# The last SwiGLU on the undivided residual with a turned result, and pools padded to multiples of 1 KB

## The chip, the cores and the metric

The kernel runs on one core of a Trainium2 chip. The metric is the device time of one execution in microseconds (us). Everything is computed in float32: the large products take their operands in a rounded form of it (fp32r below), split into a high and a low part.

## The reference

A backbone of two layers over 256 latent and 256 context tokens of 1,024 channels. Each layer is a half SwiGLU, a mixer and a second half SwiGLU. What matters here is the second SwiGLU of the last layer, for latent tokens alone, and the norm behind it:

```python
def rmsnorm(x, g):
    y = x * rsqrt(mean(x * x, axis=-1) + NORM_EPS)
    return y * g
def modulate(h, shift, scale):
    return h * (1 + scale) + shift
def swiglu(h, w_gate, w_up, w_down):
    return (silu(h @ w_gate) * (h @ w_up)) @ w_down
...
        lat = lat + m_lat[:, :, 5] * y_lat                     # y_lat: the odd mixer's out projection
        lat = lat + 0.5 * gate * swiglu(modulate(rmsnorm(lat, g), shift, scale), *ffn2)
    return rmsnorm(lat, final_norm)                            # (1, 256, 1024)
```

The inner size of a SwiGLU is 2,816, that is 22 tiles of 128.

## The kernel before, in words

Channels lie on the 128 partitions and tokens along the free dimension. The residual `res` has eight channel tiles of 512 columns: 256 context tokens (CTX), then 256 latent ones (LAT). Every product with weights goes through `mm3` (L152 to 161): for each tile of 128 input channels three matmuls, high weight by high x (L158), high weight by low x (L159), low weight by high x (L160). A column block of weights is loaded by SP into a `raw` tile, cast on ScalarE (L148) and its remainder taken on VectorE (L149). Four raw and four weight tiles rotate. The first three SwiGLU passes, the input projections and most of the rest run over 512 columns, the last SwiGLU over 256.

A SwiGLU (`ffn`, L437) first norms its input: the sum of squares over channels is kept in `acc` by `stat` (ScalarE squares, VectorE adds, L291 and L292). `rstd_stats` sums it over the partitions by a matmul with a column (L253), VectorE takes the inverse root in nine small steps (L260 to L269), and `rstd_rows` turns the two columns into a row on all partitions (matmul with the identity, L278). Then `norm_tile` makes each of the eight x tiles (L309, L314, L316), and the gate and up products follow. Inner tiles come in groups of 6, 8 and 8; behind each group `down` multiplies them by the down weights, eight blocks of output channels, and `residual` (L429) adds each block to `res`. Accumulators rotate through six banks of PSUM (`pm`), two more (`ps`) serve the norms.

`final` takes the norm's row again, multiplies each of the eight tiles by gain and row on VectorE (L1266), and sends it out on SP's queue (L1269). The result leaves with channels on partitions, (8, 128, 256), and is turned on the host.

Each engine works through its own queue in order. The order is set by a scheduler while the kernel is built, from the code's order, priorities (`high_priority`) and its own estimates. Tiles live in pools; a pool's slots lie side by side, and those of a stage (`phase`) start behind the constants, the weight tiles and the small tiles (`cst`, `rawp`, `wp`, `sm`).

Of the kernel before, what the change touches and what calls it, by code (L numbers as in the profile page):

```python
# [9 lines left out]
F32 = mybir.dt.float32  # L10
F32R = mybir.dt.float32r
I32 = mybir.dt.int32
AF = mybir.ActivationFunctionType
ALU = mybir.AluOpType
# [4 lines left out]
P = 128  # L19
D = 1024  # L20
KT = D // P
NTOK = 256
T2 = 2 * NTOK
F = 2816
NF = F // P
CHUNKS = ((0, 6), (6, 14), (14, 22))
# [7 lines left out]
SOON = 100  # L34
# [13 lines left out]
CTX, LAT = (0, NTOK), (NTOK, T2)  # L48
# [17 lines left out]
class Builder:  # L66
    def __init__(self, tc, ctx, t, out):
        self.tc, self.nc, self.t, self.out = tc, tc.nc, t, out
        pool = lambda name, bufs, **kw: ctx.enter_context(tc.tile_pool(name=name, bufs=bufs, **kw))
        self.cst = pool("cst", 1)  # L70
        self.rawp = pool("rawp", 4)
        self.wp = pool("wp", 4)
        self.sm = pool("sm", 4)
        self.pmm = pool("pmm", 6, space=PSUM)
        self.psm = pool("psm", 2, space=PSUM)
        self.dram = pool("dram", 1, space=DRAM)
        self.n = 0
        self.bg = []
        self.stage = None
        self.last_act = None  # L80
        self.keep = tc.keep_in_program_order

    def uid(self, s):
# [342 lines left out]
    def residual(self, i, ps, gate, h, last):  # L426
        c0, c1 = h
        r = self.res[:, i, c0:c1]
        self.nc.vector.scalar_tensor_tensor(  # L429
            r, ps[:, c0:c1], gate[:, i, VEC[h] : VEC[h] + 1], r, op0=ALU.mult, op1=ALU.add  # L430
        )
        if last:
            self.stat(i, h)


    def blocks(self, idx, n=3):
# [2 lines left out]
    def ffn(self, l, k, halves, after=None, spare=None, lead=None):  # L439
        nc, t = self.nc, self.t  # L440
        idx = 2 * l + k // 2
        lo, hi = halves[0][0], halves[-1][1]
        wgu = t["wgu"][idx]
        xs, pss = self.norm_proj(l, k, halves, self.blocks(idx, 4 if lead else 3), lead, spare if len(halves) > 1 else None)
        if lead is not None:
            self.mod_setup()
            self.start(self.mod_job((0, m) for m in (2, 3, 4, 5, 6, 7)), 1.6)
        for f0, f1 in CHUNKS:
            hid = []
            for f in range(f0, f1):  # L450
                for g in range(2):
                    if 2 * f + g == len(pss):
                        pss.append(self.pm())
                        w = self.wload(wgu[f, g], D)
                        self.mm3(pss[-1][:, lo:hi], self.wparts(w, KT), self.parts(xs, lo, hi))
                pg, pu = pss[2 * f : 2 * f + 2]
                s = self.slot("h", [P, 2, T2])
                nc.scalar.activation(s[:, 0, lo:hi], pg[:, lo:hi], AF.Silu)  # L458
                nc.vector.tensor_mul(s[:, 1, lo:hi], s[:, 0, lo:hi], pu[:, lo:hi])  # L459
                hd = self.slot("h", [P, 2, T2], F32R)  # L460
                self.split(hd[:, 0, lo:hi], hd[:, 1, lo:hi], s[:, 1, lo:hi])
                hid.append(hd)
                self.tick(2)
            gate = self.need(l, 3 * k + 2)
            self.down(lambda i: t["wd"][idx, i][:, f0 * P : f1 * P], hid, gate, halves, f1 == NF, f1 - f0, after)

    def proj(self, name, blk, xs, c0, c1):
        w = self.wload(self.t[name][blk], D)
        ps = self.pm()
        self.mm3(ps[:, c0:c1], self.wparts(w, KT), self.parts(xs, c0, c1))  # L470
        return ps
# [630 lines left out]
    def odd_mixer(self):  # L1102
        nc, t = self.nc, self.t
# [4 lines left out]
        xs, pss = self.norm_proj(1, 1, both, [t["od_in"][i] for i in ODD], spare="g")  # L1108
# [8 lines left out]
        for i in range(4):  # L1117
            ps = pss[i]
# [17 lines left out]
        for i in range(4):  # L1136
            ps = self.proj("od_in", 16 + i, xs, *LAT)
            nc.scalar.activation(lg[:, i], ps[:, N:T2], AF.Gelu_apprx_tanh)
        gates = {}
        for i in range(4):  # L1140
# [3 lines left out]
            for d in range(2):  # L1144
                ra = gates[i, d] = self.slot("g", [P, 2, T2])
                for g in range(2):
                    ps = self.pm()
# [100 lines left out]
        for i in range(4):  # L1248
            ps = self.pm()
            for f in range(4):  # L1250
                src = (yr if f < 2 else yi)[:, f % 2, i * P : (i + 1) * P]
                nc.tensor.matmul(ps[:, :N], lhsT=src, rhs=idft[:, f, :], start=f == 0, stop=f == 3)
            z = self.slot("hy", [P, N])
            v.scalar_tensor_tensor(z, uu[:, i], hb[:, i : i + 1], ps[:, :N], op0=ALU.mult, op1=ALU.add)
            v.tensor_mul(z, z, x0[:, i])
            o = self.slot("x", [P, 2, T2], F32R)
            self.split(o[:, 0, N:T2], o[:, 1, N:T2], z)
            os.append(o)
        self.out_proj("od_out", 1, os, [LAT])

    def final(self):
        nc = self.nc
        self.rb[LAT] = self.rstd([self.acc[LAT]], self.inv_d)
        for i in range(KT):
            y = self.slot("h", [P, NTOK])
            nc.vector.scalar_tensor_tensor(  # L1266
                y, self.res[:, i, NTOK:T2], self.gain[:, 6, i : i + 1], self.rb[LAT], op0=ALU.mult, op1=ALU.mult
            )
            nc.sync.dma_start(self.out[i], y)  # L1269

    def build(self):
        nc, t = self.nc, self.t
# [1 line left out]
        self.acc, self.rb, self.mod = {}, {}, {}  # L1274
        self.res = self.const([P, KT, T2], "res")
        s5p = dict.fromkeys(("sb0", "sb1", "pa", "pb", "bank", "tm", "mb", "mbt", "vt", "et"), 1)
        self.phase(x=8, **s5p, gs=2, sc=1, junk=1, m=2, ct=1, h=10)
        self.ct = self.slot("ct", [P, KT, 32])
        for i in range(0, KT, 2):
            nc.sync.dma_start(self.res[:, i : i + 2, :], t["xt"][:, i : i + 2, :])  # L1280
# [16 lines left out]
        for i in range(KT):  # L1297
            if i == 6:
                w = self.slot("sc", [P, 2, 4, 2 * P])
# [27 lines left out]
        self.drain()  # L1327
        self.phase(x=8, g=8, lx=2, hy=13)
        self.odd_mixer()
        self.phase(x=8, h=10)  # L1330
        self.ffn(1, 2, [LAT])
        self.final()
        self.stage.close()

# [158 lines left out]
```

## Time and profile before

| | |
|---|---|
| median of 3 runs | 1797.6 us (1797.04 to 1797.97) |
| the profiled execution | 1795.22 us, of which 1793.4 span |
| mean granted TensorE clock | 0.986 |
| TensorE busy | 1727.7 us, 96% of the span |
| VectorE busy | 1252.9 us, 70% |
| ScalarE busy | 684.1 us, 38% |
| last layer's second SwiGLU | about 1584 to 1781 us |

The span runs from the first to the last instruction; the execution's own time is 1.8 us longer. Matmuls are pipelined: one that takes 282 ns in the profile starts 119 ns after the one ahead of it, so the distance of the starts is the cost, and a busy TensorE isn't one at its peak. A line such as "PE mm L158" is the matmul of line 158 that writes a tile named mm.

### The profile page before, as it was taken

Reading aid. Unit: us, or ns where it says so; the run is one execution under the profiler, and the core shown is the slowest. Engines: PE = TensorE matmul, PEld = TensorE weight load, DVE = VectorE, ACT = ScalarE, POOL = GpSimd, SP = SyncE. Lnnn points to the kernel's source line nnn. Section 1 sums busy time; section 2 is a strip of 40 time slices with the busy share of each in tenths; the row PEclk is TensorE's granted clock in tenths of the full one; section 3 lists DMA queues with packets and bytes.
Section 4 is the critical chain, followed back from the end, with each engine's and each line's share of the span. In section 5 each row is a group of like instructions: output and inputs, shape, how many; then the busy total and the mean of one; then the engine's idle time right before and its main releaser. Section 6 shows DMA issues by size and latency. Waiting matters only on the chain.

```text
span 1793.4 us, 24725 instructions
## 1 busy us (share of the span) xinstructions
PE 1727.7 (96%) x9364; PEld 1444.7 (81%) x9364; DVE 1252.9 (70%) x2464; ACT 684.1 (38%) x1082; POOL 13.2 (1%) x47
## 2 busy tenths in 40 slices
PE   5999999999989999999999999999999999789997
PEld 3778777779868788778888888888888888589997
DVE  7999999987488668776666686544543576875555
ACT  4433333343445653222222233222122357554442
POOL 0000000000000000000000000000000000000000
PEclk9999999999998999999999999999999999799999
DMA  9566666652465453464454544555433225146552
GB/s 324 173 216 211 223 214 216 210 189 90 125 185 172 120 189 115 154 223 152 147 183 153 164 130 130 179 173 163 156 117 95 94 94 201 49 150 191 183 185 92
DMA packets 108055, 292.63 MB, mean 163 GB/s; under 512 B 21216, under 2 KB 36448, under 8 KB 107680
## 3 DMA queue, kind: packets, MB, share of 16 engines
q1 hardware_dynamic: 102368, 287.39, 49.8%
q10 hardware_dynamic: 4928, 2.10, 0.7%
q8 instruction: 73, 1.20, 0.3%
q0 software_dynamic: 640, 1.57, 0.3%
q14 instruction: 46, 0.38, 0.1%
HBM read 272.20 MB, written 18.28 MB: 162 GB/s over the span
## 4 chain that ended last, share of the span: by engine, by line
PE 87%; DVE 7%; DMA 2%; ACT 1%; issue 1%; SPq 1%; DVEq 0%; ACTq 0%
PE mm L158 25%; PE mm L160 25%; PE mm L159 25%; PE mm L155 6%; DVE w L149 1%; DMA h<-in_modw_dram 1%; PE mm L1148 1%; SPq L981 1%; DVE nt L309 1%; DMA x<-d_g 1%; DVE x L316 1%; DMA x<-d_v 0%; PE ps L278 0%; PE ps L631 0%; PE ps L1059 0%
## 5 line engine op out<-in xcount | busy, mean ns | idle before, releaser
L159 PE MATMUL mm<-x,w 128*128 128x512 f32 (+1 forms) x1600 | 575.1, 360 | 0.0
L160 PE MATMUL mm<-x,w 128*128 128x512 f32 (+1 forms) x1600 | 574.5, 360 | 0.0
L158 PE MATMUL mm<-x,w 128*128 128x512 f32 (+1 forms) x1600 | 569.4, 361 | 4.5 <-ACT x L314 3.3
L148 ACT CAST w<-raw 128x1024 fp32r<-128x1024 f32 (+2 forms) x324 | 328.5, 1018 | 527.7 <-issue 254.1
L149 DVE TENSOR_TENSOR w<-raw,w 128x1024 fp32r<-128x1024 f32 (+2 forms) x324 | 384.0, 1187 | 191.7 <-ACT w L148 190.8
L158 PEld LDWEIGHTS mm<-x,w 128*128 128x128 f32 x1600 | 300.9, 189 | 55.9 <-ACT x L314 3.9
L159 PEld LDWEIGHTS mm<-x,w 128*128 128x128 f32 x1600 | 301.8, 189 | 48.9 <-issue 2.0
L160 PEld LDWEIGHTS mm<-x,w 128*128 128x128 f32 x1600 | 301.8, 189 | 48.7 <-issue 1.2
L225 DVE CUSTOM_DVE_ANT_0 junk<-m,sc 128x1024 f32<-128x1024 f32 x224 | 273.3, 1220 | 1.8 <-DMA m<-in_modw_dram 0.2
L158 PE MATMUL mm<-h,w 128*128 128x512 f32 (+1 forms) x632 | 229.2, 367 | 0.0
L160 PE MATMUL mm<-h,w 128*128 128x512 f32 (+1 forms) x632 | 228.4, 364 | 0.0
L159 PE MATMUL mm<-h,w 128*128 128x512 f32 (+1 forms) x632 | 228.3, 363 | 0.0
L429 DVE SCALAR_TENSOR_TENSOR res<-mm,mraw,res 128x256 f32<-128x256 f32 x192 | 86.1, 480 | 103.7 <-PE mm L160 92.8
L459 DVE TENSOR_TENSOR h<-h,mm 128x512 f32<-128x512 f32 (+1 forms) x88 | 54.6, 621 | 128.5 <-PE mm L160 111.0
L458 ACT ACTIVATE h<-mm 128x512 f32<-128x512 f32 (+1 forms) x88 | 48.0, 545 | 234.5 <-PE mm L160 223.7
L159 PEld LDWEIGHTS mm<-h,w 128*128 128x128 f32 x632 | 119.1, 188 | 20.6 <-issue 1.0
L158 PEld LDWEIGHTS mm<-h,w 128*128 128x128 f32 x632 | 118.6, 188 | 21.0 <-issue 1.1
L160 PEld LDWEIGHTS mm<-h,w 128*128 128x128 f32 x632 | 118.9, 188 | 20.5 <-issue 0.6
L155 PE MATMUL mm<-x,w 128*128 128x256 f32 x384 | 66.1, 289 | 6.7 <-DVE x L316 6.2
L314 ACT ACTIVATE x<-nt,mraw 128x256 fp32r<-128x256 f32 x88 | 42.9, 506 | 54.5 <-DVE nt L309 54.5
L155 PEld LDWEIGHTS mm<-x,w 128*128 128x128 f32 x384 | 53.9, 188 | 11.6 <-DVE x L316 9.2
L165 DVE TENSOR_TENSOR h<-h,h 128x512 fp32r<-128x512 f32 (+1 forms) x88 | 54.5, 619 | 0.0
(345 smaller groups left out, 1604.5 us busy)
## 6 DMA issues: line engine op xcount, KB each, us to landing
raw<-in_wgu_dram SPq DMA_DIRECT2D x176, 512.0 KB, 3.8
m<-in_modw_dram SPq DMA_DIRECT2D x130, 512.0 KB, 4.3
raw<-in_wd_dram SPq DMA_DIRECT2D x64, 512.0 KB, 3.6
raw<-in_wd_dram SPq DMA_DIRECT2D x32, 384.0 KB, 3.3
raw<-in_od_in_dram SPq DMA_DIRECT2D x20, 512.0 KB, 3.5
h<-in_modw_dram SPq DMA_DIRECT2D x12, 512.0 KB, 9.9
raw<-in_ev_in_dram SPq DMA_DIRECT2D x10, 512.0 KB, 3.5
d_mb<-mbt SPq DMA_DIRECT2D x16, 256.0 KB, 2.9
```

The costliest lines, as they stand in the source:

```text
L148: nc.scalar.copy(hi[:, :n], raw[:, :n])
L149: nc.vector.tensor_sub(lo[:, :n], raw[:, :n], hi[:, :n])
L155: mm = lambda *a, **k: self.keep(self.nc.tensor.matmul(*a, **k))
L158: mm(ps, lhsT=wh, rhs=xh, start=first and i == 0, stop=False)
L159: mm(ps, lhsT=wh, rhs=xl, start=False, stop=False)
L160: r = mm(ps, lhsT=wl, rhs=xh, start=False, stop=last and i == n - 1)
L165: self.nc.vector.tensor_sub(lo, src, hi)
L225: nc.vector.tensor_tensor_reduce(self.junk, w, self.sc[:, v, :], 1.0, 0.0, ALU.mult, ALU.add, raw[:, dt, v : v + 1])
L314: self.last_act = nc.scalar.activation(x[:, 0, c0:c1], y, AF.Identity, bias=b)
L429: self.nc.vector.scalar_tensor_tensor(r, ps[:, c0:c1], gate[:, i, VEC[h] : VEC[h] + 1], r, op0=ALU.mult, op1=ALU.add)
L458: nc.scalar.activation(s[:, 0, lo:hi], pg[:, lo:hi], AF.Silu)
L459: nc.vector.tensor_mul(s[:, 1, lo:hi], s[:, 0, lo:hi], pu[:, lo:hi])
```

## The change

Two things change.

*The last SwiGLU.* x is no longer normed. When od_out's `residual` has made a channel tile, the tile is multiplied by its scale alone and split (`unscaled`), so x is ready tile by tile; the shift stands in two more columns beside it, and a product of 258 columns yields the gate (or up) sums of the 256 tokens and, in column 256, what the shift adds. The inverse root, which is the same for all channels of a token, is multiplied in behind the product, from a row that is copied once into `rb`. x lies in slots of the mixer's `hy` pool, and the stage isn't changed between mixer and SwiGLU.

*The end.* When the last down product has made a channel tile, it is multiplied by the gain on ScalarE and turned by TensorE, two transposes per tile, into four banks (`final_tiles`). The inverse root stays a column, and four instructions (two on VectorE, two on ScalarE) scale 512 columns each from PSUM; four transfers of 256 KB go out, two from SP's and two from ScalarE's queue. The result leaves with tokens on partitions.

*The pools.* A tile of 136 columns is put into `cst` and one of 64 into `sm`, and the pools of the first stage stand in another order.

```diff
+        for p, k in ((self.cst, 136), (self.sm, 64)):
+            p.tile([P, k], F32, tag="pad", name=f"pad{k}", bufs=1)
...
         if last:
             self.stat(i, h)
+            if self.done is not None:
+                self.done(i, h)
...
+    def ffn_last(self, l, k, xs):
+        nc, t = self.nc, self.t
+        idx = 2 * l + k // 2
+        n = NTOK
+        with self.tc.high_priority(offset=SOON):
+            rb = self.slot("g", [P, n])
+            nc.scalar.copy(rb, self.rstd([self.acc[LAT]], self.inv_d))
+        gate = self.need(l, 3 * k + 2)
+        for f0, f1 in CHUNKS:
+            hid = []
+            for f in range(f0, f1):
+                pg, pu = self.pm(), self.pm()
+                for g, ps in enumerate((pg, pu)):
+                    w = self.wload(t["wgu"][idx, f, g], D)
+                    self.mm3(ps[:, : n + 2], self.wparts(w, KT), self.parts(xs, 0, n + 2))
+                b = self.small([P, 2], "bias")
+                s = self.slot("g", [P, 2, n])
+                nc.vector.tensor_copy(b[:, 0:1], pg[:, n : n + 1])
+                nc.vector.tensor_mul(s[:, 0, :], pg[:, :n], rb)
+                nc.scalar.activation(s[:, 0, :], s[:, 0, :], AF.Silu, bias=b[:, 0:1])
+                nc.vector.tensor_copy(b[:, 1:2], pu[:, n : n + 1])
+                nc.vector.tensor_mul(s[:, 1, :], pu[:, :n], rb)
+                nc.vector.scalar_tensor_tensor(s[:, 1, :], s[:, 1, :], b[:, 1:2], s[:, 0, :], op0=ALU.add, op1=ALU.mult)
+                hd = self.slot("x", [P, 2, T2], F32R)
+                self.split(hd[:, 0, n:T2], hd[:, 1, n:T2], s[:, 1, :])
+                hid.append(hd)
+            if f1 == NF:
+                self.done = self.final_tiles()
+            self.down(lambda i: t["wd"][idx, i][:, f0 * P : f1 * P], hid, gate, [LAT], f1 == NF, f1 - f0)
+
+    def unscaled(self, l, k, xs):
...
+        def done(i, h):
+            x, r, g = xs[i], self.res[:, i, h[0] : h[1]], sc[:, i, 0:1]
+            with self.tc.high_priority(offset=SOON):
+                nc.scalar.activation(x[:, 0, :NTOK], r, AF.Copy, scale=g)
+                nc.vector.scalar_tensor_tensor(x[:, 1, :NTOK], r, g, x[:, 0, :NTOK], op0=ALU.mult, op1=ALU.subtract)
+
+        for i, x in enumerate(xs):
+            self.split(x[:, 0, NTOK : NTOK + 2], x[:, 1, NTOK : NTOK + 2], sh[:, i, 0:1].to_broadcast([P, 2]))
+        return done
...
+        self.xl = [self.slot("hy", [P, 2, T2], F32R) for _ in range(KT)]
+        self.done = self.unscaled(1, 2, self.xl)
         self.out_proj("od_out", 1, os, [LAT])
+        self.done = None
+
+    def final_tiles(self):
+        nc = self.nc
+        self.fin = [[self.pm() for _ in range(2)] for _ in range(2)]
+        def done(i, h):
+            y = self.slot("g", [P, NTOK])
+            nc.scalar.activation(y, self.res[:, i, h[0] : h[1]], AF.Copy, scale=self.gain[:, 6, i : i + 1])
+            for j in range(2):
+                nc.tensor.transpose(self.fin[j][i // 4][:, i % 4 * P : (i % 4 + 1) * P], y[:, j * P : (j + 1) * P], self.ident)
+        return done
...
-        self.rb[LAT] = self.rstd([self.acc[LAT]], self.inv_d)
-        for i in range(KT):
...
+        _, r = self.rstd_stats([self.acc[LAT]], self.inv_d)
+        for j in range(2):
+            for q in range(2):
+                y = self.slot("g", [P, T2])
+                if q:
+                    nc.scalar.activation(y, self.fin[j][q], AF.Copy, scale=r[:, j : j + 1])
+                else:
+                    nc.vector.tensor_scalar(y, self.fin[j][q], r[:, j : j + 1], None, op0=ALU.mult)
+                (nc.scalar if q else nc.sync).dma_start(self.out[j, :, q * T2 : (q + 1) * T2], y)
...
-        self.phase(x=8, **s5p, gs=2, sc=1, junk=1, m=2, ct=1, h=10)
+        self.phase(x=8, h=10, sc=1, junk=1, m=2, **s5p, gs=2, ct=1)
...
-        self.phase(x=8, h=10)
-        self.ffn(1, 2, [LAT])
+        self.ffn_last(1, 2, self.xl)
```

In the built programs the tiles that the weight products read start, counted from a multiple of 1,024 bytes: the weight tiles w at 480 before and 0 after; x at 96 before and 0 after; the inner tiles h at 864 in the first SwiGLU and 96 in the others before, 0 after.

On TensorE, where od_out's products end and the last SwiGLU begins, the order before was (mm is an accumulator, ps and acc belong to the norm, x and w to the products):

```order
L160 MATMUL mm_12945<-x_12700,w_12942 128x256
L253 MATMUL ps_13010<-inv_d,acc_12734 128x1 x2
L278 MATMUL ps_13010<-ident,rs_y_13014 128x128 x2
L158 MATMUL mm_12992<-x_12984,w_12997 128x256
L158 MATMUL mm_12993<-x_12984,w_13002 128x256
```

At the same place it is now (hy is an x tile of the last SwiGLU):

```order
L164 MATMUL mm_12985<-x_12702,w_12982 128x256
L162 MATMUL mm_13041<-hy_12705,w_13045 128x258
L163 MATMUL mm_13041<-hy_12705,w_13045 128x258
L164 MATMUL mm_13041<-hy_12705,w_13045 128x258
L162 MATMUL mm_13041<-hy_12706,w_13045 128x258
```

The column sums (now L257) stand 62 products further on, and the row products 143, two products ahead of the seventh accumulator, mm_13254:

```order
L162 MATMUL mm_13184<-hy_12712,w_13216 128x258
L282 MATMUL ps_13017<-ident,rs_y_13021 128x128 x2
L163 MATMUL mm_13184<-hy_12712,w_13216 128x258
L164 MATMUL mm_13184<-hy_12712,w_13216 128x258
L162 MATMUL mm_13254<-hy_12705,w_13258 128x258
```

In the last down product before, one block followed the other on TensorE without anything between. Now, at the end of the fifth block (mm_15211), four transposes (L1326) of the fourth and the fifth tile (g_15202, g_15240) stand between it and the sixth:

```order
L163 MATMUL mm_15211<-x_15048,w_15208 128x256
L164 MATMUL mm_15211<-x_15048,w_15208 128x256
L1326 MATMUL mm_15051<-ident,g_15202 128x128
L1326 MATMUL mm_15053<-ident,g_15202 128x128
L1326 MATMUL mm_15052<-ident,g_15240 128x128
L1326 MATMUL mm_15054<-ident,g_15240 128x128
L162 MATMUL mm_15249<-x_14551,w_15246 128x256
```

Likewise the two of the first tile, g_15088, stand directly behind the first block. The others stand within a later block, one block or more behind their own, and those of the last two behind all products. ScalarE makes g_15088 (L1324) in this place of its own order, behind the cast of the fifth block's weights (w_15208), whose slot is the one that the first block's weights had:

```order
L168 CAST x_15048<-g_15041 128x256
L152 CAST w_15208<-raw_15206 128x1024
L291 ACTIVATE acc_15086<-res 128x256
L1324 ACTIVATE g_15088<-res,gain 128x256
L152 CAST w_15246<-raw_15244 128x1024
```

Before, the same cast was followed by squares alone; the scaled copies are new.

## Rows read from the trace of the kernel before

**Rows 1.** Busy time of each engine in three stretches

```profile
core 0: us, PE busy (x) PEld busy (x) DVE busy (x) ACT busy (x) POOL busy (x), PEclk, DMA share, GB/s
50.00:400.00 350.00, 349.24 (x1629) 276.78 (x1628) 324.22 (x655) 131.46 (x203) 1.01 (x9) 1.00 0.65 205
900.00:1000.00 100.00, 100.00 (x432) 81.06 (x431) 65.22 (x97) 24.94 (x30) 0.00 (x0) 1.00 0.52 166
1595.10:1764.00 168.90, 168.90 (x1426) 168.90 (x1425) 96.58 (x126) 75.93 (x108) 0.00 (x0) 1.00 0.58 181
```

**Rows 2.** Timeline of TensorE into the last SwiGLU: start, duration, instruction, idle before

```profile
1583.59 0.28 PE L160 MATMUL mm<-x,w 128*128 128x256 f32 x1
1586.68 0.58 PE L253 MATMUL ps<-inv_d,acc 128*128 128x1 f32 x4 [2.82 <-DVE acc L292]
1589.28 1.22 PE L278 MATMUL ps<-ident,rs_y 128*128 128x128 f32 x4 [2.02 <-DVE rs_y L269]
1591.62 1.23 PE L158 MATMUL mm<-x,w 128*128 128x256 f32 x4 [1.11 <-ACT x L314]
1592.86 0.41 PE L160 MATMUL mm<-x,w 128*128 128x256 f32 x1
1593.07 0.41 PE L159 MATMUL mm<-x,w 128*128 128x256 f32 x1
```

**Rows 3.** Busy time of each engine in two stretches there

```profile
1584.00:1588.00 4.00, 0.58 (x4) 0.52 (x4) 2.54 (x7) 1.26 (x2) 0.00 (x0) 1.00 0.60 178
1588.20:1594.90 6.70, 4.50 (x19) 4.21 (x20) 5.33 (x22) 2.46 (x6) 0.00 (x0) 0.50 0.10 41
```

**Rows 4.** TensorE alone in two stretches of down products, 512 columns

```profile
387.00:407.00 20.00, 20.00 (x88) 1.00 0.58 198
886.00:906.00 20.00, 20.00 (x88) 1.00 0.56 183
```

**Rows 5.** Timeline of TensorE: a run of 512-column float32 matmuls, two transposes

```profile
1476.57 13.04 PE L1148 MATMUL mm<-lx,wg 128*128 128x512 f32 x30
...
1500.96 0.38 PE L1197 MATMUL ps<-ident,hy 128*128 128x128 f32 x2
```

**Rows 6.** Groups by line and shape, 1595 to the end: busy us, mean ns

```profile
L149 DVE TENSOR_TENSOR w<-raw,w 128x1024 fp32r<-128x1024 f32 x56 | 68.3, 1225 | 45.9 <-ACT w L148 45.9
L148 ACT CAST w<-raw 128x1024 fp32r<-128x1024 f32 x56 | 58.2, 1046 | 53.6 <-issue 31.9 <-PE mm L160 17.7 <-DMA raw<-in_wgu_dram 2.7
L429 DVE SCALAR_TENSOR_TENSOR res<-mm,mraw,res 128x256 f32<-128x256 f32 x24 | 11.3, 481 | 16.4 <-PE mm L160 16.2
L459 DVE TENSOR_TENSOR h<-h,mm 128x256 f32<-128x256 f32 x22 | 9.3, 421 | 11.3 <-PE mm L160 6.0 <-ACT h L458 5.0 <-issue 0.3
L164 ACT CAST h<-h 128x256 fp32r<-128x256 f32 x22 | 8.8, 401 | 0.0
L291 ACT ACTIVATE sq<-res 128x256 f32<-128x256 f32 x7 | 2.9, 414 | 9.5 <-DVE res L429 9.5
L261 DVE TENSOR_SCALAR rs_y<-rs_v 128x2 int32<-128x2 int32 x1 | 0.2, 169 | 0.0
```

**Rows 7.** Timeline where the mixer ends: VectorE, then TensorE

```profile
1559.51 0.44 DVE L165 TENSOR_TENSOR g<-hy,g 128x256 fp32r<-128x256 f32 x1
1559.84 0.44 DVE L1255 TENSOR_TENSOR hy<-hy,hy 128x256 f32<-128x256 f32 x1
...
1558.94 0.58 PE L159 MATMUL mm<-g,w 128*128 128x256 f32 x1 [0.48 <-DVE g L165]
```

**Rows 8.** Chain that ended last, from the last product: start, duration, what

```profile
1781.21 0.13 PE mm L160
...
1785.57 0.77 PE ps L278 x4
...
1786.36 0.48 DVE h L1266
```

**Rows 9.** Timeline of the output's issue on SP's queue

```profile
1786.87 3.78 SPq L1269 DMA_DIRECT2D out_dram<-h  x8
```

**Rows 10.** DMA's busy share (tenths) in 40 slices of 1785 to 1794

```profile
DMA  0000000000008869595959688795920000001000
```

More of the change, by code (lines that the diff above doesn't have):

```diff
@@ L465, in ffn @@
             self.down(lambda i: t["wd"][idx, i][:, f0 * P : f1 * P], hid, gate, halves, f1 == NF, f1 - f0, after)
+    def ffn_last(self, l, k, xs):
[29 more added lines that the diff above has]
+        nc = self.nc
+        sh, sc = self.mod[l, 3 * k], self.mod[l, 3 * k + 1]
+        def done(i, h):
[6 more added lines that the diff above has]
+        return done
     def proj(self, name, blk, xs, c0, c1):
@@ L1258, in odd_mixer @@
             os.append(o)
+        self.xl = [self.slot("hy", [P, 2, T2], F32R) for _ in range(KT)]
+        self.done = self.unscaled(1, 2, self.xl)
         self.out_proj("od_out", 1, os, [LAT])
+        self.done = None
+    def final_tiles(self):
+        nc = self.nc
+        self.fin = [[self.pm() for _ in range(2)] for _ in range(2)]
[5 more added lines that the diff above has]
+        return done
     def final(self):
         nc = self.nc
-        self.rb[LAT] = self.rstd([self.acc[LAT]], self.inv_d)
-        for i in range(KT):
[L1265 to L1269, printed above, removed]
+        _, r = self.rstd_stats([self.acc[LAT]], self.inv_d)
[7 more added lines that the diff above has]
+                (nc.scalar if q else nc.sync).dma_start(self.out[j, :, q * T2 : (q + 1) * T2], y)
     def build(self):
@@ L1486 @@
         aps[name] = nc.dram_tensor(f"in_{name}_dram", a.shape, mybir.dt.from_np(a.dtype), kind="ExternalInput").ap()
-    out = nc.dram_tensor("out_0_dram", (KT, P, NTOK), F32, kind="ExternalOutput").ap()
+    out = nc.dram_tensor("out_0_dram", (2, P, D), F32, kind="ExternalOutput").ap()
     with tile.TileContext(nc, schedule_with_timeline_sim=True) as tc:
@@ L1491 @@
     got = r.results[0]["out_0_dram"]
-    return np.ascontiguousarray(got.reshape(D, NTOK).T).reshape(1, NTOK, D)
+    return np.ascontiguousarray(got).reshape(1, NTOK, D)
```

## The prediction

> **What bounds the kernel now.** I read the stretch view first, then the timelines of the two places that the change rewrites, then the chain at the end. In the long products TensorE never rests: it is busy in all of 900 to 1000 and in all of 1595 to 1764 us [rows 1]. The stretch view counts every matmul that touches a stretch, so the distance of two starts is (stretch + duration) / count: (100 + 0.40) / 432 = 232.4 ns for 512 columns and (168.9 + 0.28) / 1426 = 118.6 ns for 256. VectorE is the second resource: 324.2 of 350 us in the first SwiGLU, 96.6 of 168.9 in the last [rows 1]. TensorE stands still in two places near the end. Before the last SwiGLU its last product starts at 1583.59 and the next weight product at 1591.62; in between it runs four column sums and four row products, each after a wait for VectorE [rows 2]. The granted clock is 1.00 from 1584 to 1588 and 0.50 from 1588.2 to 1594.9 [rows 3], so the first products are 213 ns apart instead of 119 [rows 2]. And after its last product at 1781.21 there are 12.1 us of norm, scaling and output [rows 8].
>
> **The sum's base.** The profiled execution took 1795.22 us, 1.8 more than its span; the median shown is 1797.6. I sum differences in the profiled one and take them from the median.
>
> **The start of the last SwiGLU.** Before, od_out's last product could have been followed at 1583.71; the last product ends at 1781.34: 197.6 us. The changed order puts gate/up products straight behind od_out's, on tiles that need neither the mean nor the row product; these stand 62 and 143 products later, behind some 7 and 17 us of cover. What remains is 1056 products of 258 columns and 528 of 256. Two columns cost 2 x (232.4 - 118.6) / 256 = 0.9 ns, so 1056 x 119.5 = 126.2 and 528 x 118.6 = 62.6: 188.8 us. Added on TensorE: the column sums (0.1 to 0.58, the row of before, taken 0.2) and four row-product passes at 0.11 (the pace of two 128-column turns, [rows 5]), 0.4. The seventh accumulator then needs a free bank: row products, ScalarE's copy into rb (0.40, [rows 6]), VectorE's bias copy (0.17) and first product with rb (0.42), less two products still running: 0.8 us of idle time. VectorE per feature tile: two weight remainders 2 x 1.23, two bias copies 2 x 0.17, two products with rb 2 x 0.42, the fused add and multiply 0.48 and the remainder 0.42 [rows 6] are 4.5 us beside 48 products of 119.5, 5.7 us: covered. If it were not, each tile would show the difference, 22 times.
>
> **The last down product.** Here the change takes something back. Two turns (0.22 us) follow each residual block; banks for them leave two for the blocks, which is enough, since a residual (0.48) is read within the next block (24 x 0.119 = 2.85). But the order puts the turns of block 0 directly behind block 0's own products, and those of block 4 directly behind block 4's. Before block 0's turns ScalarE casts a weight whose slot block 0 itself holds: 1.05, then the square 0.41, then the scaled copy 0.40 [rows 6], with two hand-overs of 0.05 it is 1.9 idle and 0.22 of turns. Behind block 4: residual 0.48, square 0.41, copy 0.40 and hand-overs, 1.4 idle, 0.22 of turns. Blocks 1, 2 and 5 cost 0.22 each. Together 4.4. The last feature tile's remainder stands behind a weight remainder on VectorE (1.23): block 0 may wait 0.3 for it. So 188.8 + 0.2 + 0.4 + 0.8 + 4.4 + 0.3 = 194.9 against 197.6: 2.7 us gained. A half clock falls away with the idle time; the idle times of 1.9 and 1.4 us are a good deal shorter than the one behind which it fell [rows 2, 3].
>
> **The end.** Until the statistics are scaled (1785.57) nothing shortens: ScalarE squares and copies, TensorE turns, +0.1. The row products (0.77) go, and eight multiplies of 0.48, the last one's transfer issued by 1790.65 [rows 9], become two on VectorE and two on ScalarE of 512 columns, about 0.65 each. The first output would be issued 0.6 us earlier; 1.05 MB moved in 4.0 us (18 slices of 0.225 us from the 13th on, [rows 10]) and still need 3.6 to 4.0, now the bound. I take 1.0 us gained (0.5 to 1.6).
>
> **The end of the mixer.** Eight pairs of two-column instructions for the shift are queued on ScalarE and VectorE among the gated casts, where VectorE runs without a gap and TensorE waits 0.48 us for it [rows 7]. The nearest row is 0.17 for 128x2, overlapped some 0.13: 1.0 us on VectorE, of which TensorE's own backlog at half clock hides part. I take +0.6 (0 to 1.5). The other reordering is in the attention part, with the same instructions: 0, with 2 either way.
>
> **The padding.** It adds no instruction on any engine. In the built program w starts 480 bytes past a multiple of 1,024, x 96, h 864 in the first SwiGLU and 96 later; after it all start at 0. With h at 864 (387 to 407 us) and at 96 (886 to 906) 20 us hold 88 products each [rows 4]; a weight slice at 480 lies inside one KB and its neighbour at 992 crosses an edge, and the starts in [rows 1] keep one average. So I cost it at 0. The trace can't exclude a gain: every one of these starts is an odd multiple of 32 bytes, none a multiple of 64. [...] Bound below: rows 4 tell two starts apart to 1 in 88, so that much of 4,872 x 232.4 + 3,312 x 118.6 ns, 17 us, could hide from them as a loss. I take 0, the value of rows 4, which are the only ones with different starts.
>
> [...]
>
> **Sum.** -2.7 - 1.0 + 0.6 + 0 = -3.1: 1792.1 in the profiled execution, 1794.5 against the median.
>
> **Rivals.** [...]
>
> [...]
>
> *Slower: the turns stall the last down product.* Place: the two spots where turns stand behind their own block. In-order queues: if VectorE has just begun a weight remainder when the block ends, the residual waits 1.23 more. With that and a late cast TensorE would rest about as long as ahead of the last SwiGLU, behind which 6.7 us ran at half [rows 3], 3.4 lost each. Both spots: -3.1 + 2 x 1.23 + 2 x 3.4 = +6.2, 1803.8. It decides where both idle times double. Against: at both spots VectorE's order has the residual ahead of the next weight remainder.
>
> **How the numbers follow.** Forecast 0.42, its own range 1791 to 1798; starts in part 0.26; fully 0.20; stalls 0.12. What a measurement tells from no change is 0.2%, 3.6 us. Faster takes both rivals of the starts and 0.18 of the forecast's 0.42: 0.64. Same: 0.22 of it and 0.02 of the stalls: 0.24. Slower 0.12. The range of 8 in 10 reaches from 1695 (half of the full rival below it, 0.10) to 1802 (about 0.07 above).
>
> **What would show it.** In the changed trace: starts 118.6 and 232.4 ns apart, or else the starts rule and I was wrong in the largest term; gate/up products directly behind od_out's with the clock at 1.00; one idle spot of 0.8 before the seventh accumulator; two of 1.9 and 1.4 in the last down product; the last output issued about 6 us after the last product. Idle spots twice as long there, with a half clock behind, make the last rival right.

## The result, and the profile after

The changed kernel takes 1778.24 us (median of 4 runs, 1777.47 to 1779.75), against 1797.32 for the kernel before in the same comparison: a ratio of 0.9895, interval 0.9878 to 0.9912. It is 19.1 us faster, where 3.1 was forecast. Its profiled execution took 1779.75 us, span 1777.6, clock 0.982.

The long stretches first, busy time of each engine as in [rows 1]: the first SwiGLU, 512-column products, the last gate and up products (258 columns) and a down product (256):

```profile
50.00:400.00 350.00, 349.09 (x1660) 282.01 (x1659) 329.64 (x666) 134.36 (x207) 0.79 (x7) 1.00 0.66 209
900.00:1000.00 100.00, 100.00 (x443) 82.84 (x442) 65.66 (x97) 26.72 (x33) 0.00 (x0) 1.00 0.53 170
1622.00:1667.00 45.00, 45.00 (x374) 45.00 (x374) 33.02 (x62) 22.67 (x31) 0.00 (x0) 1.00 0.62 193
1669.00:1690.00 21.00, 21.00 (x177) 21.00 (x176) 12.87 (x17) 7.89 (x9) 0.00 (x0) 1.00 0.59 187
```

100 us that held 432 products of 512 columns now hold 443. Over the 1,080 products from the first of the second SwiGLU pass to its first 256-column one, the starts lie 250.97 us apart before and 244.80 after: 232.4 and 226.7 ns each. The 256-column products went the other way, from 118.6 to (21.0 + 0.28) / 177 = 120.2 ns (120.0 over a whole block), and those of 258 take (45.0 + 0.28) / 374 = 121.1 (120.8). So padding wasn't free: it made one size faster and the other slower.

Where the last SwiGLU starts, the timeline of TensorE answers [rows 2]. Gate and up follow od_out after 0.12 us instead of 8.03, and the one idle spot of 0.8 us, ahead of the seventh accumulator, is there: 1586.79 less 1585.83 less one product of 0.12 is 0.84.

```profile
1567.55 0.28 PE L164 MATMUL mm<-x,w 128*128 128x256 f32 x1
1567.67 0.28 PE L162 MATMUL mm<-hy,w 128*128 128x258 f32 x1
...
1585.83 0.28 PE L164 MATMUL mm<-hy,w 128*128 128x258 f32 x1
1586.79 0.39 PE L162 MATMUL mm<-hy,w 128*128 128x258 f32 x1 [0.68 <-DVE g L493]
```

In the last down product the two idle spots stand where the prediction put them, 1.90 and 1.26 us, and behind the first the products are 0.21 us apart for a while:

```profile
1742.74 0.68 PE L1326 MATMUL mm<-ident,g 128*128 128x128 f32 x2 [1.90 <-ACT g L1324]
1743.08 0.56 PE L162 MATMUL mm<-x,w 128*128 128x256 f32 x1
1743.44 0.41 PE L163 MATMUL mm<-x,w 128*128 128x256 f32 x1
1743.65 0.41 PE L164 MATMUL mm<-x,w 128*128 128x256 f32 x1
...
1758.11 0.44 PE L1326 MATMUL mm<-ident,g 128*128 128x128 f32 x2 [1.26 <-ACT g L1324]
```

The granted clock there, in the view of stretches (the number before the last two), is 0.53 over the 3.2 us behind the first idle spot and 1.00 in the next stretch:

```profile
1743.20:1746.40 3.20, 3.20 (x18) 3.20 (x17) 0.03 (x1) 0.00 (x0) 0.00 (x0) 0.53 0.00 0
1746.50:1750.00 3.50, 3.50 (x31) 3.50 (x31) 1.77 (x3) 1.76 (x3) 0.00 (x0) 1.00 0.02 5
```

The chain at the end, to hold against [rows 8]: the last product, the last turns, the scaling, and the transfers.

```profile
1767.27 0.13 PE mm L164
...
1768.87 0.44 PE mm L1326 x2
...
1771.74 0.66 DVE g L1339
1772.40 0.66 DVEq L1558
```

From the last product's end to the end of the span it is 10.25 us instead of 12.10.

One spot that no term of the sum held appeared at the hand-over from the first SwiGLU to the mixer. TensorE, timeline:

```profile
418.37 0.52 PE L159 MATMUL mm<-h,w 128*128 128x256 f32 x3
420.74 0.38 PE L159 MATMUL mm<-x,w 128*128 128x256 f32 x1 [1.85 <-ACT x L318]
...
422.47 0.80 PE L159 MATMUL mm<-x,w 128*128 128x256 f32 x2 [1.34 <-DVE x L320]
```

Behind these waits the granted clock fell to 0.50, and it did so once more near the end of the attention:

```profile
421.90:428.60 6.70, 6.13 (x29) 6.13 (x29) 2.87 (x8) 1.52 (x3) 0.00 (x0) 0.50 0.42 144
606.20:612.90 6.70, 6.70 (x34) 5.80 (x35) 0.92 (x2) 3.89 (x8) 1.50 (x2) 0.50 0.62 147
```

In experiment 7 below, the same kernel with its pools in the old order, the clock stays at 1.00 in both places:

```profile
422.00:428.00 6.00, 5.18 (x39) 4.53 (x37) 5.23 (x18) 2.16 (x5) 0.00 (x0) 1.00 0.29 110
600.00:607.00 7.00, 5.79 (x50) 4.73 (x50) 0.46 (x2) 5.34 (x10) 1.50 (x2) 1.00 0.58 146
```

Behind the two waits the changed kernel is 3.6 us later than experiment 7, counted from the stage's start, and when the clock is back, 5.2: the waits are the larger part of the hand-over's excess, the half clock the rest.

The span in stages, each from the start of one product to that of another, in us, worked out from the traces (the other columns are experiments, below):

```
stage                                       before   after   pads  no pads  old order  turns late
                                                             only           + pads     no pads
start to the first SwiGLU's last 256-blocks  408.1   400.4  400.4   401.1    401.9     400.7
hand-over to the mixer                        41.6    47.0   45.8    41.8     41.8      41.8
even mixer and attention                     177.8   179.8  180.1   176.8    176.9     176.9
two SwiGLU passes, odd mixer to its end      928.9   912.8  912.7   912.6    912.5     912.5
od_out and what is ahead of it                27.1    27.4   27.3    26.3     26.4      26.4
od_out's last to the SwiGLU's first            8.0     0.1    8.0     0.1      0.1       0.1
to the third down product                    166.8   169.7  168.5   169.7    169.4     169.7
third down product and the end                35.1    40.2   35.9    38.9     38.8      35.3
```

The 512-column passes give 7.7 and 16.1 us; the rewritten start 7.9; the hand-over and the attention take back 7.4, the stage up to the third down product 2.9, and that down product 7.0 (22.96 to 29.99 us), of which the end returns 1.85. The stages add up to the 15.8 us between the two profiled spans; the medians are 19.1 apart, because the execution profiled before (1795.22 us) took less than the four of the comparison, and the one after the most of its four.

### The profile page after: what moved, and what is told of

It reads as the page before. It is cut to its first block, busy times and chain, and to the rows that moved or that the text cites. A ratio compares the mean times of both kernels' runs of the same rounds, so it can differ in the third digit from the quotient of the medians.

```text
span 1777.6 us, 24856 instructions
## 1 busy us (share of the span) xinstructions
PE 1716.8 (97%) x9376; PEld 1454.0 (82%) x9376; DVE 1268.6 (71%) x2546; ACT 694.9 (39%) x1101; POOL 13.2 (1%) x47
## 5 line engine op out<-in xcount | busy, mean ns | idle before, releaser
L163 PE MATMUL mm<-x,w 128*128 128x512 f32 (+1 forms) x1424 | 521.1, 366 | 0.1
L164 PE MATMUL mm<-x,w 128*128 128x512 f32 (+1 forms) x1424 | 520.1, 366 | 0.0
L162 PE MATMUL mm<-x,w 128*128 128x512 f32 (+1 forms) x1424 | 515.5, 367 | 3.6 <-ACT x L318 2.2
L162 PEld LDWEIGHTS mm<-x,w 128*128 128x128 f32 x1424 | 268.3, 190 | 49.9 <-ACT x L318 2.5
L163 PEld LDWEIGHTS mm<-x,w 128*128 128x128 f32 x1424 | 269.7, 189 | 44.6 <-issue 2.0
L164 PEld LDWEIGHTS mm<-x,w 128*128 128x128 f32 x1424 | 269.5, 189 | 43.6 <-issue 1.2
L162 PE MATMUL mm<-h,w 128*128 128x512 f32 x456 | 178.3, 394 | 0.0
L164 PE MATMUL mm<-h,w 128*128 128x512 f32 x456 | 176.9, 390 | 0.0
L163 PE MATMUL mm<-h,w 128*128 128x512 f32 x456 | 176.7, 390 | 0.0
L465 DVE TENSOR_TENSOR h<-h,mm 128x512 f32<-128x512 f32 x66 | 45.3, 686 | 107.5 <-PE mm L164 95.1
L464 ACT ACTIVATE h<-mm 128x512 f32<-128x512 f32 x66 | 39.5, 598 | 193.7 <-PE mm L164 182.9
L162 PEld LDWEIGHTS mm<-h,w 128*128 128x128 f32 x456 | 85.6, 188 | 19.0 <-issue 1.1
L163 PEld LDWEIGHTS mm<-h,w 128*128 128x128 f32 x456 | 85.7, 188 | 18.3 <-issue 1.0
L164 PEld LDWEIGHTS mm<-h,w 128*128 128x128 f32 x456 | 85.6, 188 | 18.4 <-issue 0.6
L162 PE MATMUL mm<-hy,w 128*128 128x258 f32 x352 | 99.3, 284 | 0.7 <-DVE g L493 0.7
L164 PE MATMUL mm<-hy,w 128*128 128x258 f32 x352 | 99.7, 284 | 0.0
L163 PE MATMUL mm<-hy,w 128*128 128x258 f32 x352 | 99.6, 284 | 0.0
```

What stands on the lines that cost most here:

```text
L162: mm(ps, lhsT=wh, rhs=xh, start=first and i == 0, stop=False)
L163: mm(ps, lhsT=wh, rhs=xl, start=False, stop=False)
L164: r = mm(ps, lhsT=wl, rhs=xh, start=False, stop=last and i == n - 1)
```

## Experiments

The first question was what made products faster that the change doesn't touch: the starts, or the new order of instructions. The second, what the 5.7 ns per product depend on.

**1. Pads and pool order alone.** On the kernel before:

```diff
+        self.cst.tile([P, 136], F32, tag="pad", name="pad136", bufs=1)
+        self.sm.tile([P, 96], F32, tag="pad", name="pad96", bufs=1)
-        self.phase(x=8, **s5p, gs=2, sc=1, junk=1, m=2, ct=1, h=10)
+        self.phase(x=8, h=10, sc=1, junk=1, m=2, **s5p, gs=2, ct=1)
```

> The kernel before with the pads and the pools' new order alone: x, h and w start at multiples of 1 KB, the last SwiGLU and the end are the old ones. Theory 'starts': the products' pace hangs on where their operands start, so it becomes that of the changed kernel, 226.7 ns for 512 columns and 120.0 for 256, against 232.4 and 118.7. 4,872 x 5.7 = 27.8 us less and 3,312 x 1.3 = 4.3 more, and the first SwiGLU keeps about 6 back: about 1780 us (1776 to 1784). Rival 'order': the new pace comes with the rewritten SwiGLU or the new order of instructions; then 232.4 and 118.7 stay and it takes 1797 us (1795 to 1799).

Measured: 1780.56 us, ratio 0.9909 (0.9894 to 0.9923), 226.7 and 120.0 ns. The view of stretches:

```profile
900.00:1000.00 100.00, 100.00 (x443) 82.84 (x442) 66.42 (x98) 26.75 (x33) 0.00 (x0) 1.00 0.53 169
```

Pads without a single new instruction give the whole new pace. The first part of "starts" holds.

**2. The changed kernel without pads and in the old order of pools.**

> The changed kernel without pads and with the pools' old order: the new last SwiGLU and the new end on starts at odd multiples of 32 bytes. Theory 'starts': 232.4 and 118.7 ns are back, and what is left is the rewritten part: 8.0 us gained where the last SwiGLU starts, 1.9 behind the last product, 7 lost in the last down product and 1 to 2 for 258 columns: 1795 us (1792 to 1799). Rival 'order': 226.7 and 120.0 ns and about 1779 us.

Measured: 1769.18 us, ratio 0.9848 (0.9831 to 0.9864), 9 us faster than the changed kernel, and neither theory's number:

```profile
900.00:1000.00 100.00, 100.00 (x443) 82.79 (x442) 62.84 (x90) 26.46 (x33) 0.00 (x0) 1.00 0.50 161
```

The new pace is there without the pads. But the rival isn't right either: the new code's small bias tiles take 128 bytes ahead of the stages, so x moved from 96 to 224 past a multiple of 1 KB, while w stayed at 480. 224 less 480 is -256; in the changed kernel x less w is 0; in the kernel before 96 less 480 is -384. What the fast ones share is a distance of a multiple of 256 bytes between the moving tile and the weights.

**3 and 4. One operand at a time.** The kernel before with the new pool order and other pads: first w at 0 and x, h at 96, then x, h at 0 and w at 480.

```diff
+        self.cst.tile([P, 136], F32, tag="pad", name="pad136", bufs=1)
+        self.sm.tile([P, 120], F32, tag="pad", name="pad120", bufs=1)
```

> The kernel before with the pools' new order and other pads: w starts at a multiple of 512 bytes, x and h 96 bytes past a multiple of 1 KB. If the starts of the weights decide: 226.7 and 120.0 ns, about 1780 us. If those of the moving operand decide: 232.4 and 118.7 ns, about 1797 us. If each has a share: 512 columns between 227 and 232 ns, and the two shares of this kernel and of the one with x and h alone add up to 5.7.

```diff
+        self.sm.tile([P, 232], F32, tag="pad", name="pad232", bufs=1)
```

> The complement: x and h start at multiples of 1 KB, w 480 bytes past a multiple of 512. If the starts of the moving operand decide: 226.7 and 120.0 ns, about 1780 us. If those of the weights decide: 232.4 and 118.7 ns, about 1797 us. I lean to the moving operand: each product fetches 512 columns of it and 128 of w, and w is fetched beside the product ahead.

Measured: 1808.96 us (ratio 1.0068, 1.0053 to 1.0083) with w alone, 1799.54 (1.0016, 1.0007 to 1.0026) with x and h alone. Neither operand decides, and the shares don't add up: at 512 columns both are slower than before (252.00 us for the 1,080 products, 233.3 ns). Two stretches of the first, 512 columns and the last SwiGLU:

```profile
900.00:1000.00 100.00, 100.00 (x430) 80.47 (x429) 67.23 (x101) 25.46 (x30) 0.00 (x0) 1.00 0.51 161
1680.00:1760.00 80.00, 80.00 (x669) 80.00 (x668) 45.10 (x55) 34.44 (x48) 0.00 (x0) 1.00 0.59 185
```

And of the second, 512 columns and one down product of the last SwiGLU:

```profile
900.00:1000.00 100.00, 100.00 (x430) 80.32 (x429) 66.62 (x99) 24.40 (x29) 0.00 (x0) 1.00 0.51 165
1696.00:1717.00 21.00, 21.00 (x183) 21.00 (x182) 13.11 (x16) 7.88 (x9) 0.00 (x0) 1.00 0.63 197
```

With 256 columns they part: (80 + 0.28) / 669 = 120.0 ns at a distance of 96, (21 + 0.28) / 183 = 116.3 at 32 (116.7 by the starts of a whole block). So the distance matters for both sizes, and what is good for one size isn't for the other.

**5. All distances in one kernel.**

```diff
-        xs = [self.slot("x", [P, 2, T2], F32R) for _ in range(KT)]
+        xs = [self.slot("x", [P, 2, T2 + 8], F32R) for _ in range(KT)]
-                hd = self.slot("h", [P, 2, T2], F32R)
+                hd = self.slot("h", [P, 2, T2 + 8], F32R)
```

> The kernel before with the first pads (w at multiples of 512 bytes), the pools' old order, and x and h tiles of 2 x 520 columns in place of 2 x 512, so that the starts of x and h differ from tile to tile and go through all multiples of 32 bytes within 512. Every product's distance to the next is read by the start of its x or h. Theory 'distance': not the start itself but the distance between x's start and w's, taken modulo 256 bytes, sets the pace (fast runs so far: 0 and 256; slow: 32, 96, 128): two classes, 227 ns at distances 0 and 256 and 232 to 234 ns at the other fourteen, so about 1797 us. Rival 'multiple of 128 or less': 64 and 192 or more of them are fast too. Rival 'gradual': the pace rises step by step with the distance from a multiple of 256, largest at 128.

Measured: 1793.62 us. From the trace, the mean of the distance between two starts by the start of the first one's x or h (above) modulo 512, 178 to 579 products each:

```
  0   32   64   96  128  160  192  224 |  256  288  320  352  384  416  448  480
229.9 234.0 234.4 229.2 232.8 232.2 229.7 235.4 | 229.6 234.2 234.4 229.3 232.5 231.8 229.6 235.3 ns
```

The two halves agree within 0.4 ns: the period is 256 bytes. But there are no two classes and no slope, and 0 takes 229.8 here where it takes 226.7 in the changed kernel. The high and low halves of a tile lie 32 bytes apart in this kernel, so hardly any product follows one with the same start; from 96 to 64 it was 229.3, from 64 to 96 235.3. The few that do, 44 at a start of 0, still took 229.3. So the neighbours' starts count too, and this table doesn't hold for uniform starts.

**6. The turns one block later.** On the version of experiment 2:

```diff
-            for j in range(2):
-                nc.tensor.transpose(self.fin[j][i // 4][...], y[:, j * P : (j + 1) * P], self.ident)
+            turns = [(self.fin[j][i // 4][...], y[:, j * P : (j + 1) * P]) for j in range(2)]
+            for p, q in self.late:
+                self.keep(nc.tensor.transpose(p, q, self.ident))
+            self.late = turns
```

The matmuls of the last down product are kept in the code's order as well, and `final` issues the last two turns.

> The changed kernel without pads and with the pools' old order (1769.2 us), and the turns of each tile one block later in TensorE's order. If the two idle times of 1.9 and 1.4 us in the last down product go and nothing takes their place: 1766.0 us (1765 to 1767.5). If the turns' wait is only moved to another block, or hidden work now stands in the open: 1768.5 to 1770. If the later turns prolong the end, slower than 1770.

Measured: 1766.68 us, ratio 0.9833 (0.9818 to 0.9847), 2.5 less than without it. No wait is left at the turns, the first ones now behind the second block:

```profile
1732.95 1.60 PE L156 MATMUL mm<-x,w 128*128 128x256 f32 x12
1734.39 0.38 PE L1325 MATMUL mm<-ident,g 128*128 128x128 f32 x2
1734.52 2.75 PE L156 MATMUL mm<-x,w 128*128 128x256 f32 x21
```

The third down product and the end went from 38.9 to 35.3 us (table above). Both waits came from the order, not from the turns themselves.

**7. Pads with the old order of pools.** The changed kernel with one line put back.

> The changed kernel with its pads, but the pools of the first stage in the old order. Both x and h still lie a multiple of 256 bytes from w. Theory 'pool order': with h second, the next stage's x tiles lie where the last down product still reads h, the hand-over from the first SwiGLU to the mixer takes some 5 us more, and the attention behind it 2 to 3 more; in the old order both go: 1770 us (1768 to 1773), 227 and 120.0 ns as in the changed kernel. Rival 'pads': the multiples of 1 KB themselves cost the 9 us between the changed kernel and the one without pads; then 1778 stays.

Measured: 1769.98 us, ratio 0.9851 (0.9834 to 0.9867): 8.3 less than the changed kernel. h starts at 768 past a multiple of 1 KB here, and the 1,080 products still take 244.80 us: no multiple of 1 KB is needed. The hand-over is back at 41.8 and the attention at 176.9.

**8. Pool order alone.** The kernel before with that one line changed and no pads.

> The kernel before with the pools' new order and no pads, nothing else: x and w keep their distance of 128, so 232.4 and 118.7 ns stay. Theory 'pool order': the hand-over from the first SwiGLU to the mixer takes 45 to 47 us in place of 41.7, and the attention up to 2 more: 1803 us (1800 to 1806). Rival: the hand-over is longer only where pads are there too: 1797 us.

Measured: 1801.74 us, ratio 1.0028 (1.0018 to 1.0039), 45.7 for the hand-over and 179.7 for the attention. The 1,080 products take 250.97 us as before. TensorE waits in the same two places and as long as in the changed kernel:

```profile
429.14 0.38 PE L155 MATMUL mm<-x,w 128*128 128x256 f32 x1 [1.85 <-ACT x L314]
430.87 0.39 PE L155 MATMUL mm<-x,w 128*128 128x256 f32 x1 [1.34 <-DVE x L316]
```

The mixer's first x tile lies at byte 130,144 of a partition in both. In the new order h's first slot is at 130,144 too; in the old one h begins at 183,392. The tile in that slot is one that the last down block's products read. ScalarE wrote the x tile while h was still being read before (products of h run to 426.5 there), and here only behind them. The first row is of the kernel before, the second of this one, after the last product of h at about 427.0:

```profile
424.31 0.49 ACT L314 ACTIVATE x<-nt,mraw 128x256 fp32r<-128x256 f32 x1
```

```profile
428.60 0.49 ACT L314 ACTIVATE x<-nt,mraw 128x256 fp32r<-128x256 f32 x1
```

By the built program's addresses, though, the last product that reads this slot ended at 425.9, and ScalarE stood idle for 1.23 us ahead of 427.33; in its queue the x tile comes behind two weight casts, of 425.06 and 427.33. That the scheduler put it there because of the shared slot fits all this and isn't shown.

The attention is 2 to 3 us longer as well in all five kernels with the new order (178.6 to 180.1). In the changed kernel the clock is 0.50 behind the waits of the hand-over and again near the attention's end (above), and 64-column products are 0.21 us apart in that second stretch instead of 0.11. In this one it is 0.96 on average from 400 to 440 us, where the kernel before and experiment 7 have 1.00. What makes the clock fall there, no run shows.

**9. Uniform distances of 64, 160, 192 and 224**, by pads inside the stages of experiment 6's version:

```diff
+        self.phase(pd=1, x=8, ..., ct=1, pe=1, h=10)
+        self.slot("pd", [P, 16])
+        self.slot("pe", [P, 24])
...
+        self.phase(pd=1, x=8, sc=1, junk=1, m=3, y=7, pe=1, h=10)
+        self.slot("pd", [P, 48])
+        self.slot("pe", [P, 8])
```

> The same version with pads inside the stages, so that within a stage all x tiles have one distance from w and all h tiles another, modulo 256: 64 for x and 160 for h in the first SwiGLU, 192 for x and 224 for h in the next two. It completes the table of uniform distances for 512 columns (so far 226.7 at 0, 233.3 at 32 and 96, 232.4 at 128). If 0 alone is fast: 231 ns or more at all four, and about 1785 us. If the pace by tile in the kernel with mixed distances holds for uniform ones: 234.4 at 64, 232.0 at 160, 229.7 at 192, 235.4 at 224, about 1780 us.

Measured: 1789.34 us. Stretches at 64, 160, 192 and 224 in turn:

```profile
342.00:372.50 30.50, 30.50 (x134) 25.03 (x134) 26.76 (x51) 12.32 (x21) 0.11 (x1) 1.00 0.71 221
387.00:407.00 20.00, 20.00 (x87) 16.05 (x86) 19.28 (x37) 10.54 (x17) 0.00 (x0) 1.00 0.60 205
800.00:880.00 80.00, 80.00 (x344) 64.13 (x343) 48.01 (x67) 21.71 (x28) 0.00 (x0) 1.00 0.49 154
885.00:924.00 39.00, 39.00 (x169) 31.41 (x168) 28.76 (x46) 7.36 (x7) 0.00 (x0) 1.00 0.51 172
```

All distances between two starts in these places have means of 229.5, 234.2, 233.3 and 233.3 ns. For 512 columns 0 is the fastest of the eight, as the first theory had it, though 64 misses its bound of 231. The paces by tile of experiment 5 miss at all four, by some 2 ns at 160 and 224 and by 4 to 5 at 64 and 192.

**10 to 12. The last stage at 32, 192 and 64**, where only products of 256 and 258 columns run:

```diff
-        self.phase(x=8, g=8, lx=2, hy=13)
+        self.phase(pd=1, x=8, g=8, lx=2, hy=13)
+        self.slot("pd", [P, 8])
```

> The version with the turns a block later (1766.7 us), and a pad of 32 bytes ahead of the pools of the last stage, so that its x, g and hy tiles start 32 bytes past a multiple of 256 from w; the 512-column products of the other stages keep their distance of 0. Theory 'distance': 256 columns take 116.3 ns at 32 (the run with x and h alone on multiples of 1 KB) against 120.0 at 0, and 258 columns follow: 1,584 x 3.7 = 5.9 us in the last SwiGLU and some 2 in the mixer: 1759 us (1757 to 1762). If 258 columns don't follow: 1762 to 1764. If the distance isn't what sets the pace: 1766.7 and 120.0 ns.

> As the version with 32 bytes ahead of the last stage's pools (1762.3 us; 256 columns 117.0 ns and 258 columns 120.0 there), with 192 bytes in their place. Uniform 256-column products at 192 took 116.5 ns in the kernel with uniform starts. If 258 columns follow those of 256 at this distance, they take some 117.4 and it is 3 us faster: 1759.5 us. If 258 columns always cost what they did at 0 and 32, 120 to 121 ns: 1762 us again.

> The same with 64 bytes. No run has uniform 256-column products at 64; those of mixed starts took 117.6 ns there. If the distance acts on 256 and 258 columns alike: 117.6 and 118.5 ns and 1761 us. If 258 columns keep 120 or more: 1762 to 1764 us. If 64 is no better than 0: 1766.7 us.

Measured: 1762.28 us at 32 (ratio 0.9805, 0.9792 to 0.9818), 1761.71 at 192 (0.9804, 0.9791 to 0.9817), 1765.43 at 64 (0.9822, 0.9809 to 0.9835). Stretches of a down product (256 columns) and of gate and up (258), at 32, then at 192:

```profile
1660.00:1680.00 20.00, 20.00 (x174) 20.00 (x173) 12.43 (x17) 7.86 (x9) 0.00 (x0) 1.00 0.60 187
1683.00:1726.00 43.00, 43.00 (x361) 43.00 (x360) 31.23 (x60) 21.66 (x30) 0.00 (x0) 1.00 0.60 181
```

```profile
1659.00:1679.00 20.00, 20.00 (x179) 20.00 (x178) 12.88 (x16) 7.30 (x8) 0.00 (x0) 1.00 0.60 201
1683.00:1725.00 42.00, 42.00 (x350) 42.00 (x349) 30.89 (x57) 21.05 (x30) 0.00 (x0) 1.00 0.59 186
```

By the starts, over a whole block or stage, 256 columns go from 120.0 to 116.7 and 113.4 ns; 258 go from 120.8 to 120.0 and stay at 120.8. So the two columns more don't follow the 256, and the gain at 32 is 4.4 us where 7.7 was expected. The version at 192 has the lowest median, 35.2 us below the kernel before and 16.5 below the changed one, but not clearly below the one at 32.

Uniform distances, in ns (256 and 258 columns as far as a clean stretch shows them):

```
x less w, modulo 256     0      32     64     96    128    160    192    224
512 columns            226.7  233.3  229.5  233.3  232.4  234.2  233.3  233.3
256 columns            120.0  116.7  117.8  120.0  118.7    -    113.4    -
258 columns            120.8  120.0  122.2    -      -      -    120.8    -
```

The distance alone doesn't fix the pace of the shorter products. In the version at 192, 256-column products, all at this distance, change pace behind two turns that stand among them:

```profile
1476.34 0.28 PE L159 MATMUL mm<-x,w 128*128 128x256 f32 x1
...
1477.05 0.28 PE L159 MATMUL mm<-x,w 128*128 128x256 f32 x1
1477.17 0.38 PE L1247 MATMUL ps<-ident,hy 128*128 128x128 f32 x2
...
1477.97 0.28 PE L159 MATMUL mm<-x,w 128*128 128x256 f32 x1
...
1478.31 0.28 PE L159 MATMUL mm<-x,w 128*128 128x256 f32 x1
```

The first two rows are six products apart, 118 ns each, the last two three, 113. By the starts it is 113.3 ns from 1477.9 to 1482.6 us and 117.8 from 1483.0 to 1488.5. The kernel before has 120.0 ns from 1045 to 1055 us and 118.7 from 408 to 418, both at 128; experiment 7 has 120.0 and 120.8 for 258 columns at 0. What switches it, no run shows.

## Why the prediction was right in direction and wrong in size

**The padding** is the step that failed: "So I cost it at 0." At the paces measured it was worth 4,872 x 5.7 = 27.8 us at 512 columns and cost about 2,256 x 1.4 + 1,056 x 1.3 = 4.5 at the others. The reason given was [rows 4]: h at 864 and at 96 run at the same pace, so starts don't matter. Those two starts differ by 768, three times 256: they are the same start modulo 256, and the weights' two, 480 and 992, are too. Every row shown of before was at one distance, 128. The argument had no second point and took that for a flat line. Of the chances, the 0.26 for "starts in part" came nearest: the starts matter, with 5.7 of 232.4 ns at 512 columns. But no multiple of 1 KB is needed for that: experiment 2 has 226.7 ns with x at 224 and w at 480, and 256 columns got slower.

That the forecast had the right direction was luck. Its 3.1 us were to come from the rewritten parts; experiment 1, which has none of them, is already 15.7 us faster than the kernel before. What is left for the rewriting, 1780.56 less 1778.24, is 2.3 us, and the intervals of the two ratios overlap. The range held the result only because it reached down to the rivals.

Pads move a 512-column product from 232.4 to 226.7 ns with the instructions unchanged (experiment 1; the pools' order alone leaves 232.4, experiment 8). The next product's weights are loaded while a product runs: before, a product of 0.28 us starts at 1565.90, and the load for the one behind it, 0.19 us, at 1565.91. That it is the two reads that meet, and where, no run shows.

**"Fully"** has 0.20 of the chances, and the range starts at 1695 on its account. Both stand on the author's estimate of what the starts could be worth, and no run shows so much: the fastest uniform paces measured are 226.7 ns for 512 columns and 113.4 for 256, 5.7 and 5.2 less than before, and the version with the lowest median is 35.2 us below the kernel before. In the first SwiGLU, where VectorE is busy for 324.2 of 350 us [rows 1], 31 products more fit into the stretch (1,660 against 1,629): 7.2 of some 8.5 us came through.

**The pools' order** has no term of its own; the nearest is the "other reordering" in the attention part, "0, with 2 either way", since the instructions are the same. The order costs 8.3 us in the changed kernel and 4.8 alone, most of it at the hand-over, which the sum left out. The instructions were counted, and where their tiles lie wasn't.

**The start of the last SwiGLU** went as worked out: products directly behind od_out's, 0.84 us idle where 0.8 was said, nothing missing on VectorE. Its products were taken at 118.6 and 119.5 and cost 120.0 and 120.8: 2.1 us more.

**The last down product.** 1.90 and 1.26 us where 1.9 and 1.4 were forecast, at the two blocks named. The half clock was denied ("a good deal shorter") and came behind the first: 1.5 us, the difference of 29.7 to the 28.2 of experiments 2 and 7, where the clock stayed. Six pairs of turns stand ahead of the last product where five were counted, some 0.2: the fourth tile's pair was left out. From first to last product it came to 199.7 instead of 194.9; products, clock and turns make some 3.8 of these 4.8, and the rest isn't traced. The rival "stalls" had the half clock once instead of twice, and no doubled idle times.

**The end** gave 1.85 us, a little more than the 0.5 to 1.6. The output moved in less time than the bound of 3.6 that was set: 1.05 MB in 11 busy slices of 0.25 us instead of the 18 of 0.225 [rows 10]. DMA's busy share in 40 slices of 1768 to 1778:

```profile
DMA  0000000000000000000008999999999500000000
```

**The end of the mixer** took 0.4 us more, and 0.6 were forecast for the shift's instructions. That isn't shown to be theirs: experiment 1, which hasn't got them, took 27.3 us there, the changed kernel 27.4, and experiments 2, 6 and 7, which have them, 26.3 to 26.4.

## What to carry to other kernels

When something in the profile runs at a pace that no wait explains, look what all its rows have in common before calling a candidate excluded: two rows that differ by a multiple of an unknown period are one row. Where a product's operands start is worth a sweep by pads of 32 bytes, per size of product, because in these runs the distance between the two operands moved the pace (226.7 to 234.2 ns for 512 columns) and no single one fitted all sizes (0 was the fastest for 512 columns, 192 for 256). And when pools are moved, ask which tiles of the next stage now lie on those that the last work of this stage still reads, and look at the granted clock behind every wait that this adds (0.50 here, behind waits of 1.85 and 1.34 us).

## What the runs showed of the hardware that was not expected

In these kernels the pace of an fp32r product on TensorE changed with the distance of its moving tile from the weights: 226.7 to 234.2 ns for 512 columns, 113.4 to 120.0 for 256. A period of 256 bytes was seen at 512 columns (226.7 ns in experiments 2 and 7, halves within 0.4 ns in 5). The neighbours' starts counted as well (229.3 ns from 96 to 64, 235.3 from 64 to 96), and at 256 columns one distance, 192, had both 113.3 and 117.8 ns. Two columns more cost 7.4 ns at 192 (113.4 against 120.8) and 0.8 at 0 (120.0 against 120.8).

Behind the same idle time of 1.90 us the granted clock was 0.53 in the changed kernel and 1.00 in experiment 7, whose instructions there are the same. The two rows are of experiment 7:

```profile
1734.41 0.44 PE L1326 MATMUL mm<-ident,g 128*128 128x128 f32 x2 [1.90 <-ACT g L1324]
```

```profile
1734.80:1738.00 3.20, 3.20 (x29) 3.20 (x28) 0.33 (x2) 0.19 (x1) 0.00 (x0) 1.00 0.00 0
```

What decides between them stays open.
